# Score products of two attention maps as two half-height matmuls, in a one-core encoder layer

## The chip, the cores and the metric

The kernel runs on one NeuronCore of a Trainium2 chip; the other cores are idle. A core has TensorE (PE, matrix products; its weight loads are shown as PEld), VectorE (DVE), ScalarE (ACT), GpSimd (POOL) and SyncE (SP, which here only issues transfers). They run side by side, each through its own list of instructions in a fixed order, and wait for one another by semaphores. Matmul results land in PSUM, eight banks of 512 float32 columns for each of 128 partitions; everything else lies in SBUF, also with 128 partitions. The metric is the device time of one execution in microseconds (us), the median of several runs.

## The reference, cut to what matters

The program is one encoder layer on 1024 tokens of 1024 channels, in float32. A normalised input is projected to pooling channels and to queries, keys and values of 8 heads; a pooling branch and an attention branch are gated and merged, projected out and added; an MLP of width 4096 follows. The change lies in the attention branch, where each head has two softmax maps with their own 64-wide queries and keys and a common 128-wide value:

```python
qn = head_rmsnorm(q, g_q) * (HEAD_DIM ** -0.5)       # [.., 8 heads, 2 maps, 64]
kn = head_rmsnorm(k, g_k)
s = einsum('bqhid,bkhid->bihqk', qblk, kn)            # i: the map
s = where(allowed, s - slopes * dist, neg)            # block-causal, ALiBi
p = softmax(s, axis=-1)
a = p[:, 0] - lam * p[:, 1]
o = einsum('bhqk,bkhe->bqhe', a, vf)
```

## The kernel before, in words

**Digits.** Matrix products are made from fp32r operands, a rounded form of float32. To keep float32 accuracy, each operand is split into a high digit (a rounded copy, ScalarE) and a low digit (the rest, a VectorE or GpSimd subtraction). `mm3` (lines 114 to 119) adds up three products: high by high, high by low, low by high.

**Scores.** Map m of a head has 64 channels, and TensorE contracts over 128 rows, so a score product uses the rows twice. `stage_qkT` (444 to 466) transposes queries and keys of one tile of 128 tokens and puts digits on top of each other. For map 0, rows 0 to 63 are its own half and 64 to 127 the other; for map 1 it is the reverse. K holds the key's high digit on the own half (line 459) and its low digit on the other (460). Q holds two variants: variant 0 has the query's high digit on the own half (461) and its low digit on the other (462); variant 1 has the low digit on the own half (463) and the high digit on the other (464). One pass with variant 0 gives high by high plus low by low; a second with variant 1, into the same PSUM bank, gives low by high plus high by low.

`stage_scores` (468 to 517) goes over query tile t of head h. It has (t+1) x 128 keys, in chunks of up to 512, so one chunk for t below 4 and two above. For each map and each chunk it takes a PSUM bank `sc` (pool `ps_s`, two banks), runs the two passes (490 and 491), and evicts with one VectorE operation (493) which adds the distance penalty and keeps the running minimum. When all chunks of a map are there, ScalarE takes the exponential of the whole row (501). There are 8 heads, 8 tiles, 96 chunks, 192 score banks and 384 score matmuls. A chunk of 128 keys is streamed twice over, so the widths are 512, 384 and 256.

**Order.** The attention stage is a software pipeline. `ORDER` (48, 49) gives each stage an offset in steps; the loop at 636 to 655 takes one piece of each stage generator in turn and then runs them out. The pieces are QKV projection (A, `z`), normalisation (B), transposes (C, `tk`), scores (D, `sc`), transposes of the attention matrix (E, `ta`), the product with values (F, `po`), the small sums of squares (H) and a per-head norm (R, `trr`). The `yield` statements inside `stage_scores` set where its pieces end. Projections for gates (`g`) and pooling (`u`), written after the loop, serve as filler. The framework's scheduler then fixes each engine's list from these priorities and its own estimate of time; it may put other matmuls between two that stand next to each other in the source.

**What else uses part of the array.** Two kinds of matmul in this kernel have a weight of fewer than 128 rows or columns: the transposes of the small parameters at line 375 (`cols_ps`, 32 rows, once) and of the norm factors at line 602 (`trr`, 8 columns, once a head).

Of the kernel before, what the change touches and what calls it, by code (L numbers as in the profile page):

```python
# [11 lines left out]
AF = mybir.ActivationFunctionType  # L12
ALU = mybir.AluOpType
# [4 lines left out]
P = 128  # L18
# [5 lines left out]
HD = 64  # L24
# [4 lines left out]
BIG = 3.0e38  # L29
# [26 lines left out]
def encoder_kernel(  # L56
# [21 lines left out]
    nc = tc.nc  # L78
    x, out = x[0], out[0]
# [17 lines left out]
    def htile(shape, dt, name, th):  # L97
        return hpools[th].tile(shape, dt, tag="H", name=name)

    def ut(shape, dt, name):  # L100
        return up.tile(shape, dt, tag="U", name=name)
# [4 lines left out]
    def f(ap):  # L106
        return ap.bitcast(F32)
# [172 lines left out]
    with ExitStack() as ph:  # L280
# [83 lines left out]
        dist = sp.tile([P, S], F32, name="dist")  # L364
# [79 lines left out]
        def stage_qkT(h, t):  # L444

            th, c0 = t // 4, (t % 4) * P
            K, qn = KV[h][0][th], st[h, t]["qn"]
            tr = ps_t.tile([P, 512], F32, tag="tr", name=f"tk{h}_{t}")
            for i in range(2):
                nc.tensor.transpose(  # L450
                    tr[:, i * P : (i + 1) * P], qn[:, 2 * i : 2 * i + 2, :].rearrange("p a b -> p (a b)"), identf
                )
            Q = sp.tile([P, 2, 2, P], F32R, tag="Q", name=f"Q{h}_{t}", bufs=N_Q)
            halves = (slice(0, HD), slice(HD, P))
            for m in range(2):
                own, other = halves[m], halves[1 - m]
                q, k = tr[own, 0:P], tr[own, P : 2 * P]
                k_hi, q_hi = K[own, m, c0 : c0 + P], Q[own, m, 0, :]
                nc.scalar.copy(k_hi, k)
                nc.vector.tensor_tensor(K[other, m, c0 : c0 + P], k, f(k_hi), op=ALU.subtract)  # L460
                nc.scalar.copy(q_hi, q)  # L461
                nc.vector.tensor_tensor(Q[other, m, 0, :], q, f(q_hi), op=ALU.subtract)
                nc.vector.tensor_tensor(Q[own, m, 1, :], q, f(q_hi), op=ALU.subtract)  # L463
                nc.scalar.copy(Q[other, m, 1, :], q)  # L464
            st[h, t]["Q"] = Q
            yield

        def stage_scores(h, t):

            K, Q = KV[h][0], st[h, t]["Q"]  # L470
            n = (t + 1) * P
            if t < 4:
                sb = ut([P, 2, 512], F32, f"s{h}_{t}")
                s = [sb[:, 0, :], sb[:, 1, :]]
            else:
                s = [ut([P, S], F32, f"s{h}_{t}_{i}") for i in range(2)]
            nm = sp.tile([P, 2, 2], F32, tag="nm", name=f"nm{h}_{t}", bufs=3)
            Z = Zs[h]
            o0 = S - P - P * t
            for i in range(2):  # L480
                last = None
                for c in range(0, n, 512):
                    w = min(512, n - c)
                    sc = ps_s.tile([P, 512], F32, tag="sc", name=f"sc{h}_{t}_{i}_{c}")
                    rhs = K[c // 512][:, i, 0:w]
                    dst = sc[:, 0:w]
                    if w == P:
                        rhs = rhs.unsqueeze(1).broadcast_to([P, 2, P])
                        dst = sc[:, 0 : 2 * P].rearrange("p (a b) -> p a b", a=2)
                    nc.tensor.matmul(dst, Q[:, i, 0, :], rhs, start=True, stop=False)  # L490
                    nc.tensor.matmul(dst, Q[:, i, 1, :], rhs, start=False, stop=True)  # L491
                    acc = nm[:, i, c // 512 : c // 512 + 1]
                    nc.vector.tensor_tensor_reduce(  # L493
                        out=s[i][:, c : c + w], in0=sc[:, 0:w], in1=dist[:, o0 + c : o0 + c + w],
                        scale=2.0 ** -(h + 1), scalar=BIG if last is None else last,
                        op0=ALU.add, op1=ALU.min, accum_out=acc,
                    )
                    last = acc
                    if c + 512 < n:
                        yield  # L500
                nc.scalar.activation(  # L501
                    s[i][:, 0:n], s[i][:, 0:n], AF.Exp, bias=last, scale=-1.0, accum_out=Z[:, i, t : t + 1]
                )
                if i == 0:
                    yield

            cf = sp.tile([P, 1], F32, tag="cf", name=f"cf{h}_{t}", bufs=3)
            nc.vector.reciprocal(cf, Z[:, 1, t : t + 1])
            nc.vector.scalar_tensor_tensor(cf, cf, Z[:, 0, t : t + 1], nlam, op0=ALU.mult, op1=ALU.mult)
            nc.vector.scalar_tensor_tensor(  # L510
                s[0][:, 0:n], s[1][:, 0:n], cf, s[0][:, 0:n], op0=ALU.mult, op1=ALU.add
            )
            if (h, t) == (H - 1, NT - 1):

                nc.vector.tensor_scalar(zero, Z[:, 1, t : t + 1], 0.0, None, op0=ALU.mult)
            st[h, t]["a"] = s[0]
            yield
# [93 lines left out]
        def stage(w, g):  # L611
            h, t = divmod(g, NT)
            if w == "A":
                if t == 0:
                    head_start(h)
                yield from stage_qkv(h, t)
            elif w == "B":
                yield from stage_prep(h, t)
            elif w == "C":
                yield from stage_qkT(h, t)  # L620
            elif w == "D":
                yield from stage_scores(h, t)
            elif w == "E":
                yield from stage_aT(h, t)
            elif w == "F" and t % 2:
                yield from stage_pv(h, t // 2)
            elif w == "H" and t % 2:
                yield from stage_ssq(h, t // 2)
            elif w == "R" and t == NT - 1:
                yield from stage_norm(h)  # L630
            elif w == "W" and t == 0 and h:
                for kp in range(NK // 2):
                    load_w(h, kp)
                    split_w(h, kp, nc.gpsimd)

        for g in range(-2, N + 8):
# [11 lines left out]
            for tok in ORDER:  # L648
                if tok not in gens:
                    i = g - tok[1]  # L650
# [145 lines left out]
    for d in range(NK):  # L796
# [3 lines left out]
        for th in range(2):  # L800
# [5 lines left out]
            t = htile([P, 2, 512], F32R, f"mT{d}_{th}", th)  # L806
# [446 lines left out]
```

## Time and profile before

| | |
|---|---|
| median of 3 runs | 1582.8 us (1582.48 to 1592.09) |
| the profiled execution | 1589.36 us, its span 1587.6 us |
| granted TensorE clock | 0.992 of full speed |
| TensorE busy | 1551.9 us (98%) |
| VectorE busy | 1008.6 us (64%) |
| ScalarE busy | 812.1 us (51%) |
| GpSimd busy | 347.8 us (22%) |
| first score pass, line 490 | 192 matmuls |
| deleted VectorE line 462 | 128 operations, 37.0 us busy |

All rows but the first two come from one profiled execution. A span reaches from the first instruction to the last; the execution's own time is a little longer. A row of the order of time gives start, duration, engine, line, operation, output and inputs, then rows and columns of the weight (128*128), then the output's shape. Matmuls overlap on TensorE: the next starts before the one ahead has ended, so the time that a matmul takes from the engine is the distance from its start to the next one's, and the sum of durations is more than the time. A weight load (PEld) usually starts together with the matmul ahead of the one that it belongs to. Helper lines stand for many callers: L111 and L112 are the two halves of a split, L117 to L119 the three products of `mm3`; the tile names tell which.

### The profile page before, as it was taken

How to read it: one execution, taken by the hardware profiler on the slowest of the kernel's cores; microseconds unless marked ns; L12 is line 12 of the kernel's file. 1: busy time of each engine (PE TensorE's matmuls, PEld its weight loads, DVE VectorE, ACT ScalarE, POOL GpSimd, SP SyncE). 2: the span in 40 equal slices, each digit the busy share in tenths (PEclk: the TensorE clock that was granted, in tenths of full speed). 3: DMA queues.
4: the chain of work that ended last, by engine and by line, in shares of the span. 5: the costliest groups of instructions: out<-in, count | busy, mean ns of one | idle time of the engine just before them, and what ended most of it. 6: DMA issues, size and time to landing. Idle time of an engine off the chain costs nothing.

```text
span 1587.6 us, 21976 instructions
## 1 busy us (share of the span) xinstructions
PE 1551.9 (98%) x7649; PEld 1328.8 (84%) x7649; DVE 1008.6 (64%) x2265; ACT 812.1 (51%) x1776; POOL 347.8 (22%) x447
## 2 busy tenths in 40 slices
PE   7999999999999999998999998999999899999999
PEld 6998999999999989887888886888888678888887
DVE  6777777777878787645221468666666568545662
ACT  6656565655665565545332456555556533333331
POOL 5424242425343433212743100000000000000000
PEclk9999999999999999999999998999999999999999
DMA  7111111111111121258527334444434699536751
GB/s 224 51 53 54 54 54 56 43 54 57 53 58 52 57 74 57 81 177 273 153 83 216 138 124 128 163 149 153 157 121 152 234 353 354 166 119 225 218 174 39
DMA packets 166393, 206.41 MB, mean 130 GB/s; under 512 B 10037, under 2 KB 102922, under 8 KB 166282
## 3 DMA queue, kind: packets, MB, share of 16 engines
q1 hardware_dynamic: 148874, 177.71, 34.6%
q10 hardware_dynamic: 17408, 27.30, 4.6%
q8 instruction: 60, 0.98, 0.3%
q14 instruction: 51, 0.42, 0.1%
HBM read 150.42 MB, written 54.56 MB: 129 GB/s over the span
## 4 chain that ended last, share of the span: by engine, by line
PE 88%; DVE 4%; DMA 4%; ACT 1%; issue 1%; POOL 1%; SPq 1%; ACTq 0%; DVEq 0%; POOLq 0%
PE z L117 5%; PE z L119 5%; PE z L118 5%; PE Da L117 4%; PE Da L118 4%; PE Da L119 4%; PE g L118 3%; PE g L117 3%; PE g L119 3%; PE Db L118 3%; PE Db L119 3%; PE Db L117 3%; PE X L117 3%; PE X L118 3%; PE X L119 3%; PE sc L490 2%
## 5 line engine op out<-in xcount | busy, mean ns | idle before, releaser
L119 PE MATMUL z<-wqkv,hT 128*128 128x384 f32 x512 | 174.3, 341 | 0.7 <-DVE hT L112 0.7
L117 PE MATMUL z<-wqkv,hT 128*128 128x384 f32 x512 | 174.7, 341 | 0.4 <-DVE qn L432 0.3
L118 PE MATMUL z<-wqkv,hT 128*128 128x384 f32 x512 | 173.6, 339 | 0.0
L501 ACT ACTIVATE s<-s,nm 128x256 f32<-128x256 f32 (+7 forms) x128 | 99.6, 778 | 48.8 <-DVE nm L493 43.4
L240 POOL TENSOR_TENSOR ms<-ms,mhalf 128x4 f32<-128x4 f32 x64 | 67.6, 1056 | 157.6 <-DVE ms L239 138.5
L119 PE MATMUL g<-hT,fwgate 128*128 128x512 f32 x256 | 101.0, 394 | 0.0
L118 PE MATMUL g<-hT,fwgate 128*128 128x512 f32 x256 | 101.0, 394 | 0.0
L117 PE MATMUL g<-hT,fwgate 128*128 128x512 f32 x256 | 100.9, 395 | 0.0
L117 PEld LDWEIGHTS z<-wqkv,hT 128*128 128x128 f32 x512 | 96.8, 189 | 4.2 <-DVE qn L432 1.3
L119 PEld LDWEIGHTS z<-wqkv,hT 128*128 128x128 f32 x512 | 96.6, 189 | 3.4 <-DVE hT L112 1.5
L118 PEld LDWEIGHTS z<-wqkv,hT 128*128 128x128 f32 x512 | 96.8, 189 | 2.9
L493 DVE CUSTOM_DVE_ANT_0 s<-sc,dist 128x512 f32<-128x512 f32 (+3 forms) x128 | 74.7, 586 | 22.1 <-PE sc L491 20.7
L112 POOL TENSOR_TENSOR wqkv<-rqkv,wqkv 128x384 fp32r<-128x384 f32 x60 | 63.2, 1071 | 20.2 <-ACT wqkv L111 19.2
L490 PE MATMUL sc<-K,Q 128*128 128x512 f32 (+2 forms) x192 | 67.2, 355 | 0.1
L491 PE MATMUL sc<-K,Q 128*128 128x512 f32 (+2 forms) x192 | 66.6, 354 | 0.0
L112 DVE TENSOR_TENSOR AS<-s,AS 128x512 fp32r<-128x512 f32 x64 | 43.7, 689 | 31.4 <-ACT AS L111 31.4
L464 ACT CAST Q<-tk 64x128 fp32r<-64x128 f32 x128 | 33.2, 259 | 58.7 <-DVE Q L463 56.8
L438 POOL TENSOR_TENSOR qn<-qn,ggh 128x128 f32<-128x128 f32 x64 | 32.4, 506 | 137.6 <-DVE qn L432 119.4
L461 ACT CAST Q<-tk 64x128 fp32r<-64x128 f32 x128 | 33.0, 258 | 50.7 <-DVE K L460 49.2
L112 POOL TENSOR_TENSOR fwgate<-frgate,fwgate 128x512 fp32r<-128x512 f32 x32 | 45.3, 1418 | 53.0 <-ACT fwgate L111 52.9
L1009 ACT ACTIVATE u<-u 128x512 f32<-128x512 f32 x64 | 40.5, 632 | 31.4 <-DVE u L823 30.3
L119 PEld LDWEIGHTS g<-hT,fwgate 128*128 128x128 f32 x256 | 48.1, 188 | 8.6
(428 smaller groups left out, 4662.8 us busy)
## 6 DMA issues: line engine op xcount, KB each, us to landing
wd<-in_w_down_dram SPq DMA_DIRECT2D x56, 512.0 KB, 5.3
wu<-in_w_up_dram SPq DMA_DIRECT2D x32, 512.0 KB, 4.4
udS<-us SPq DMA_DIRECT2D x64, 256.0 KB, 2.1
ur<-udS SPq DMA_DIRECT2D x32, 512.0 KB, 3.4
rqkv<-in_w_in_dram SPq DMA_DIRECT2D x64, 192.0 KB, 3.0
ud<-u ACTq DMA_DIRECT2D x48, 256.0 KB, 2.0
ur<-ud SPq DMA_DIRECT2D x24, 512.0 KB, 8.3
frgate<-in_w_gate_dram SPq DMA_DIRECT2D x32, 256.0 KB, 2.8
```

Of the source, the lines that this page charges most:

```text
L112: (lo_eng or nc.vector).tensor_tensor(lo, src, f(hi), op=ALU.subtract)
L117: nc.tensor.matmul(ps, lhs_hi, rhs_hi, start=first, stop=False, **kw)
L118: nc.tensor.matmul(ps, lhs_hi, rhs_lo, start=False, stop=False, **kw)
L119: nc.tensor.matmul(ps, lhs_lo, rhs_hi, start=False, stop=last, **kw)
L240: nc.gpsimd.tensor_tensor(dst, dst, mhalf[:, :n], op=ALU.pow)
L461: nc.scalar.copy(q_hi, q)
L464: nc.scalar.copy(Q[other, m, 1, :], q)
L490: nc.tensor.matmul(dst, Q[:, i, 0, :], rhs, start=True, stop=False)
L491: nc.tensor.matmul(dst, Q[:, i, 1, :], rhs, start=False, stop=True)
L493: nc.vector.tensor_tensor_reduce(out=s[i][:, c : c + w], in0=sc[:, 0:w], in1=dist[:, o0 + c : o0 + c + w], scale=2.0 ** -(h + 1), scalar=B ...
L501: nc.scalar.activation(s[i][:, 0:n], s[i][:, 0:n], AF.Exp, bias=last, scale=-1.0, accum_out=Z[:, i, t : t + 1])
L1009: nc.scalar.activation(r, r, AF.Relu)
```

## The change

`stage_qkT` no longer writes the query's low digit on the other half of variant 0, so that half of the tile stays unused. `stage_scores` turns its loops inside out: for each chunk it takes both maps' PSUM banks, issues the high-by-high products of both maps as matmuls over 64 rows each (map 0 on rows 0 to 63, map 1 on rows 64 to 127), then both maps' full-height second passes, then both evictions. The product of the two low digits is no longer computed. The pieces of the generator change too: a piece now holds both maps of a chunk, and there is a `yield` after every chunk, the last included.

```diff
@@ stage_qkT
                 nc.scalar.copy(q_hi, q)
-                nc.vector.tensor_tensor(Q[other, m, 0, :], q, f(q_hi), op=ALU.subtract)
                 nc.vector.tensor_tensor(Q[own, m, 1, :], q, f(q_hi), op=ALU.subtract)
@@ stage_scores
-            for i in range(2):
-                last = None
-                for c in range(0, n, 512):
-                    w = min(512, n - c)
+            last = [None, None]
+            for c in range(0, n, 512):
+                w = min(512, n - c)
+                scs, rhs, dst = [], [], []
+                for i in range(2):
                     sc = ps_s.tile([P, 512], F32, tag="sc", name=f"sc{h}_{t}_{i}_{c}")
...
-                    nc.tensor.matmul(dst, Q[:, i, 0, :], rhs, start=True, stop=False)
-                    nc.tensor.matmul(dst, Q[:, i, 1, :], rhs, start=False, stop=True)
+                for i, own in enumerate((slice(0, HD), slice(HD, P))):
+                    nc.tensor.matmul(dst[i], Q[own, i, 0, :], rhs[i][own], start=True, stop=False)
+                for i in range(2):
+                    nc.tensor.matmul(dst[i], Q[:, i, 1, :], rhs[i], start=False, stop=True)
+                for i in range(2):
                     acc = nm[:, i, c // 512 : c // 512 + 1]
                     nc.vector.tensor_tensor_reduce(
...
-                    last = acc
-                    if c + 512 < n:
-                        yield
+                    last[i] = acc
+                yield
+            for i in range(2):
                 nc.scalar.activation(
-                    s[i][:, 0:n], s[i][:, 0:n], AF.Exp, bias=last, scale=-1.0, accum_out=Z[:, i, t : t + 1]
+                    s[i][:, 0:n], s[i][:, 0:n], AF.Exp, bias=last[i], scale=-1.0, accum_out=Z[:, i, t : t + 1]
                 )
```

In the changed file the half-height matmuls are line 494, the full-height ones 496, the evictions 499.

More of the change, by code (lines that the diff above doesn't have):

```diff
@@ L479, in stage_scores @@
             o0 = S - P - P * t
-            for i in range(2):
-                last = None
-                for c in range(0, n, 512):
-                    w = min(512, n - c)
+            last = [None, None]
[3 more added lines that the diff above has]
+                for i in range(2):
                     sc = ps_s.tile([P, 512], F32, tag="sc", name=f"sc{h}_{t}_{i}_{c}")
-                    rhs = K[c // 512][:, i, 0:w]
-                    dst = sc[:, 0:w]
+                    r, d = K[c // 512][:, i, 0:w], sc[:, 0:w]
@@ L487, in stage_scores @@
                     if w == P:
[L488 to L491, printed above, removed]
+                        r = r.unsqueeze(1).broadcast_to([P, 2, P])
+                        d = sc[:, 0 : 2 * P].rearrange("p (a b) -> p a b", a=2)
@@ L492, in stage_scores @@
+                    scs.append(sc)
+                    rhs.append(r)
+                    dst.append(d)
+                for i, own in enumerate((slice(0, HD), slice(HD, P))):
[3 more added lines that the diff above has]
+                for i in range(2):
                     acc = nm[:, i, c // 512 : c // 512 + 1]
@@ L493, in stage_scores @@
                     nc.vector.tensor_tensor_reduce(
-                        out=s[i][:, c : c + w], in0=sc[:, 0:w], in1=dist[:, o0 + c : o0 + c + w],
-                        scale=2.0 ** -(h + 1), scalar=BIG if last is None else last,
+                        out=s[i][:, c : c + w], in0=scs[i][:, 0:w], in1=dist[:, o0 + c : o0 + c + w],
+                        scale=2.0 ** -(h + 1), scalar=BIG if last[i] is None else last[i],
                         op0=ALU.add, op1=ALU.min, accum_out=acc,
                     )
-                    last = acc
```

## The prediction

> **What bounds the kernel now.** I read the page's summary and chain first, then a table of busy time by stretch over the attention stage, then the list of TensorE's own waits there, and last the order of time around single instructions.
>
> ```profile
> span 1587.6 us, 21976 instructions
> PE 1551.9 (98%) x7649; PEld 1328.8 (84%) x7649; DVE 1008.6 (64%) x2265; ACT 812.1 (51%) x1776; POOL 347.8 (22%) x447
> ...
> PE 88%; DVE 4%; DMA 4%; ACT 1%; issue 1%; POOL 1%; SPq 1%; ACTq 0%; DVEq 0%; POOLq 0%
> ```
>
> TensorE is busy 98% of the span and holds 88% of the chain that ended last. That is an average over stages, and the change touches one stage only, that of the score matmuls (first row below: count, shortest, median and longest in ns, first and last start in us). The row after it is the sum of seven stretches, 40 to 670 us; then come the only waits of TensorE of which the trace knows between 45 and 670 us (columns: total us, times, longest).
>
> ```profile
> L490 PE MATMUL sc<-K,Q x192: 276/389/501, 49.1 to 668.7; 128*128 128x512 f32 x96, 128*128 128x256 f32 x64, 128*128 128x384 f32 x32
> ```
>
> ```profile
> sum 630.00, PE 627.77 PEld 576.05 DVE 478.37 ACT 379.61 POOL 235.12; mean PE 89.68 PEld 82.29 DVE 68.34 ACT 54.23 POOL 33.59
> ```
>
> ```profile
> PE ta L546 <- DVE AT_0l L112: 0.9, 1, 0.9
> PE ta L546 <- DVE AT_4l L112: 0.6, 1, 0.6
> PE z L117 <- DVE qn L432: 0.3, 1, 0.3
> ```
>
> Of 630 us, TensorE is without work for 2.2 us, and its waits for others are 1.8 us. VectorE is busy 478 of the 630. So in this stage a microsecond more or less on TensorE is a microsecond of the end, and work taken from VectorE or ScalarE can give back no more than about 2 us.
>
> A busy row is not the price of a matmul, since one overlaps the next; the price is the distance from start to start. The page's order of time shows it (start, duration, line):
>
> ```profile
> 409.83 0.40 PE L118 MATMUL u<-hT,fwpool 128*128 128x512 f32 x1
> 410.06 0.28 PE L490 MATMUL sc<-K,Q 128*128 128x256 f32 x1
> 410.18 0.28 PE L491 MATMUL sc<-K,Q 128*128 128x256 f32 x1
> 410.30 0.40 PE L119 MATMUL u<-hT,fwpool 128*128 128x512 f32 x1
> 410.54 0.39 PE L117 MATMUL u<-hT,fwpool 128*128 128x512 f32 x1
> ```
>
> ```profile
> 402.19 0.33 PE L117 MATMUL z<-wqkv,hT 128*128 128x384 f32 x1
> 402.37 0.33 PE L118 MATMUL z<-wqkv,hT 128*128 128x384 f32 x1
> ```
>
> A 512-column matmul takes 0.23 us of TensorE, a 384-column one 0.18, a 256-column one 0.12.
>
> **The change, part by part.**
>
> *The first passes.* Groups of the first score pass by shape, and below them the VectorE operation that the change deletes:
>
> ```profile
> L490 PE MATMUL sc<-K,Q 128*128 128x512 f32 x96 | 38.9, 405 | 0.1
> L490 PE MATMUL sc<-K,Q 128*128 128x256 f32 x64 | 18.3, 285 | 0.0
> L490 PE MATMUL sc<-K,Q 128*128 128x384 f32 x32 | 10.9, 342 | 0.0
> ...
> L462 DVE TENSOR_TENSOR Q<-tk,Q 64x128 fp32r<-64x128 f32 x128 | 37.0, 289 | 20.2 <-ACT Q L461 17.1
> ```
>
> These 192 cost 96 x 0.23 + 32 x 0.18 + 64 x 0.12 = 35.5 us. Afterwards there are still 192, of the same widths, on half of the rows. A half-height matmul streams as many columns, so by itself it saves nothing; only two of them side by side save one, at most 17.7 us in all.
>
> Whether they stand side by side is decided by the scheduler, not by the source line. In the built program of the changed kernel TensorE's list reads, at a typical place (L494 is the half-height pass, L496 the full-height one; names are tile, map, chunk):
>
> ```
> L494 sc_5_0_0  128x512      map 0, half height
> L496 sc_5_0_0  128x512      map 0, full height
> L118, L119, L117, L118 z    128x384
> L494 sc_5_1_0  128x512      map 1, half height
> L496 sc_5_1_0  128x512
> ```
>
> I went through the whole list: in none of the 96 pairs is map 0's half-height matmul followed at once by map 1's of the same chunk. Three times map 1's stands next to map 0's of the following chunk (widths 256, 384 and 256 at the narrower one); that can save 0.12 + 0.18 + 0.12 = 0.4 us. The other 186 stand alone between full-height matmuls. So there are 189 excursions from the full array into the 64-row form and back; in the kernel before there is one such excursion by rows (32 rows, L375) and eight by columns (8 of 128, L602).
>
> *What an excursion costs.* The trace has one by rows. hps are transposes, cols_ps is the 32-row one, g the next full-height matmul; PEld rows are weight loads.
>
> ```profile
> 39.77 0.60 PE L266 MATMUL hps<-identf,hn 128*128 128x128 f32 x4
> ```
>
> ```profile
> 40.09 0.27 PE L266 MATMUL hps<-identf,hn 128*128 128x128 f32 x1
> ...
> 40.29 0.13 PEld L375 LDWEIGHTS cols_ps<-identf,rows 32*128 32x128 f32 x1 [0.17 <-issue]
> 40.30 0.24 PE L375 MATMUL cols_ps<-identf,rows 32*128 32x32 f32 x1
> ...
> 40.47 0.19 PEld L118 LDWEIGHTS g<-hT,fwgate 128*128 128x128 f32 x1
> 40.47 0.50 PE L118 MATMUL g<-hT,fwgate 128*128 128x512 f32 x1
> 40.57 0.19 PEld L119 LDWEIGHTS g<-hT,fwgate 128*128 128x128 f32 x1
> 40.80 0.39 PE L119 MATMUL g<-hT,fwgate 128*128 128x512 f32 x1
> ```
>
> Transposes follow each other at (0.60 - 0.27)/3 = 0.11 us. Elsewhere a weight load starts with the matmul ahead of it; here L375's starts 0.20 us after the last hps, 0.17 of it idle with nothing waited for, and L118's load starts 0.17 after L375's matmul, although both streams had work. L118's matmul truly begins at about 40.57, where the load behind it starts, 0.10 after its own load. From the last hps to L119 are 0.71 us; at the usual distances (0.11 + 0.11 + 0.23) they would be 0.45. **This excursion cost 0.26 us.**
>
> Among transposes the weight load is already in the open, half of each 0.11. Among wide matmuls it is hidden, and an excursion uncovers it twice. By steps: a transpose streams 128 columns in about 0.06 (a quarter of 0.23), so the load came 0.14 after the stream's end; then the matmul 0.01 (as recorded for L375) to 0.10 (as for L118) after its load. That makes 0.15 to 0.24 on the way in and 0.24 on the way out, 0.39 to 0.48; measured from the usual slot in place of the stream's end (0.09 late) it is 0.10 to 0.19 and 0.19, 0.29 to 0.38. The ends are 0.26 and 0.48; I take **0.36**, the middle, since three kinds of neighbour are mixed: 149 excursions follow ordinary wide matmuls, 35 transposes or the small sums, 5 a second score pass.
>
> The other bound is the column form, with eight cases and no loss at all (the first of them in PE rows, the count of all, then its PEld rows):
>
> ```profile
> 156.45 0.34 PE L118 MATMUL z<-wqkv,hT 128*128 128x384 f32 x1
> 156.63 0.27 PE L602 MATMUL trr<-identf,r 128*8 128x128 f32 x1
> 156.74 0.49 PE L546 MATMUL ta<-identf,s 128*128 128x128 f32 x3
> ```
>
> ```profile
> L602 PE MATMUL trr<-identf,r x8: 270/271/273, 156.6 to 702.6; 128*8 128x128 f32 x8
> ```
>
> ```profile
> 156.46 0.09 PEld L602 LDWEIGHTS trr<-identf,r 128*8 128x8 f32 x1
> 156.63 0.36 PEld L546 LDWEIGHTS ta<-identf,s 128*128 128x128 f32 x3
> ```
>
> The small load starts 0.01 after the matmul ahead of it, the next one with trr itself, and the distances are the usual 0.18 and 0.11; the other seven go the same way. So the floor is nothing, the ceiling 0.48. The half-height matmul is cut by rows like L375, so I go by that row. The Trainium skill's page "TensorEngine Tiling (Array Packing)", section Key Properties, says that a change of tiling mode, not only of tile, drains TensorE. This case's trace agrees for the 32-row form (0.17 us idle) and not for the 8-column one (0.01 us); by that sentence read for all forms the sum would stay as it is.
>
> *Sum.* 189 x 0.36 = 68.0 us more, less 0.4 for the three neighbours: **+67.6 us**. The profiled execution was 1589.4 us (span 1587.6 and 1.8 around it), which would become 1657; on the median of 1582.8, which the verdict uses, 1650.
>
> *VectorE's deleted operation.* 128 x 0.289 = 37 us leave an engine with 152 us free in this stage. TensorE has no wait that names Q, so I count nothing, at most 2 us. In a stage 68 us longer VectorE has more room still, so nothing there covers less than before.
>
> *Both maps' score banks at once.* There are two sc banks. In the source the four matmuls of a chunk now precede both evictions, so the next chunk's map 0 waits for an eviction:
>
> ```profile
> L493 DVE CUSTOM_DVE_ANT_0 s<-sc,dist 128x512 f32<-128x512 f32 x80 | 54.8, 686 | 8.0 <-PE sc L491 6.9
> ```
>
> The 32 tiles of more than 512 keys have a second chunk. As the list is built, z, g or po matmuls stand between the halves and cover an eviction of 0.69 us; uncovered it would be 32 x 0.69 = 22 us, with g, z and po queued behind it on TensorE. I take nothing. DMA queues are as before: the change issues no transfer and moves none past another.
>
> **The rivals.**
>
> *Free switch (not slower).* A 64-row weight load is pulled ahead as trr's was, and the 64-row matmul fits between its neighbours. Then TensorE does the same 0.23, 0.18 and 0.12 slots as before: 1582.8 - 0.4 and up to 2 for VectorE, 1580 to 1583. For it speak the eight trr rows; against it the one row case, which is the nearer shape. It decides from the switch: below 16/189 = 0.08 us an excursion, the change is inside 1%.
>
> *Side by side (faster).* If halves ran together and switches were free, 17.7 us would go: 1565. The Trainium skill's "TensorE: Matmul & The Clock Gate", section "Measured speedup vs the span model", gives for tiles in different row groups one matmul's time plus about 4 ns each; no run here shows that yet. In this kernel it needs neighbours, and the list has three.
>
> *Small switch.* 64 rows drain less than 32 rows did, 0.08 to 0.24 us: 1598 to 1628.
>
> *Larger switch or bank waits.* Drain of 0.36 and the 22 us of evictions, or a drain of over 0.48 because the full load time (0.19 in the rows) stands in the open: 1672 to 1690.
>
> **How the numbers follow.** Drain by rows, 0.26 to 0.48 an excursion (1632 to 1673): 0.66. Small switch (1598 to 1628): 0.12. Free switch: 0.11. Larger: 0.08. Side by side: 0.03. A range of 1605 to 1680 holds the first, most of the small switch and part of the larger one, some 0.8. This kernel's measurement tells about 1% (16 us) from no change. Faster by over 1%: side by side, 0.03. Within: the free switch, 0.11. Slower: the rest, 0.86.
>
> **What would show it.** Right: L494's weight load starts 0.3 to 0.4 us after the matmul ahead of it, not with it; the load after L494 likewise; the start-to-start distance around an L494 of 512 columns is 0.5 to 0.7 us for the two steps where it was 0.46; the stage's stretch to the last score is some 68 us longer and the rest as long as before; VectorE's busy time is 37 us less. Wrong: loads of L494 that start with the matmul ahead; a stage of the same length; TensorE waits on L499's evictions (VectorE s) of more than a few us.

## The result, and the profile after

The changed kernel takes 1661.8 us (1661.3 to 1662.0) where the kernel before takes 1582.7 us: a ratio of 1.0485, 95% interval 1.0456 to 1.0513. It is 79 us slower. The profiled executions, 1661.34 and 1589.36 us, differ by 72 us, because that of before lies 7 us above its own median.

The summary of the changed kernel's page:

```profile
span 1659.6 us, 21851 instructions
PE 1619.9 (98%) x7649; PEld 1326.5 (80%) x7649; DVE 962.2 (58%) x2137; ACT 815.9 (49%) x1776; POOL 343.0 (21%) x447
```

TensorE has as many matmuls as before and is again "98% busy", 68 us more of it. That row can't tell work from a switch: a matmul that lasts longer counts as busy (a first pass of 512 columns 0.49 us in the rows below, 0.40 in the mean of before). The row of the weight loads (PEld) can: its busy time stayed (1328.8 us before, 1326.5 now) while the span grew, so its share fell from 84% to 80%. VectorE lost 128 instructions and 46 us, 37 of them those of line 462.

Next, one stretch of each kernel, from 40 us to the first matmul of the next stage (`bp`, which starts at 701.5 us before and at 777.1 us after); first the kernel before, then the changed one. The columns are the stretch, its length, and busy time with the number of instructions for each engine.

```profile
40.00:701.50 661.50, 659.27 (x3773) 602.66 (x3772) 493.65 (x1564) 397.00 (x1137) 240.28 (x328) 1.00 0.19 60
```

```profile
40.00:777.00 737.00, 734.27 (x3768) 602.59 (x3768) 444.39 (x1430) 399.96 (x1133) 236.28 (x327) 1.00 0.17 54
```

The same matmuls (both pages count 7649; the few that differ here fell over the edge of the stretch), with the same weight-load time to 0.1 us, at the same clock, take 75.5 us longer. The rest of the program, from the first `bp` to the end, went from 886.1 to 882.5 us. So the loss lies in the attention stage alone.

Inside the stage it shows up in the weight loads' idle time. From the list of waits of the changed kernel (total us, times, longest):

```profile
PEld sc L494 <- issue: 22.3, 90, 0.4
PEld sc L496 <- issue: 14.9, 65, 0.4
```

"Issue" means that the trace knows of nothing that was waited for. The two rows hold 155 of these gaps; the others stand in small rows under the names of other engines, so the price is read from single places. One place, in order of time, TensorE first and its weight loads second:

```profile
258.08 0.34 PE L117 MATMUL z<-wqkv,hT 128*128 128x384 f32 x1
258.25 0.34 PE L118 MATMUL z<-wqkv,hT 128*128 128x384 f32 x1
258.52 0.49 PE L494 MATMUL sc<-K,Q 64*128 64x512 f32 x1
258.94 0.50 PE L496 MATMUL sc<-K,Q 128*128 128x512 f32 x1
259.28 0.28 PE L117 MATMUL po<-AT_0h,V 128*128 128x256 f32 x1
```

```profile
258.08 0.19 PEld L118 LDWEIGHTS z<-wqkv,hT 128*128 128x128 f32 x1
258.52 0.18 PEld L494 LDWEIGHTS sc<-K,Q 64*128 64x128 f32 x1 [0.25 <-issue]
258.94 0.19 PEld L496 LDWEIGHTS sc<-K,Q 128*128 128x128 f32 x1 [0.24 <-issue]
259.05 0.19 PEld L117 LDWEIGHTS po<-AT_0h,V 128*128 128x128 f32 x1
```

L118's load starts with L117's matmul, as everywhere. L494's does not start with L118's matmul at 258.25 but at 258.52, and L496's not with L494's but 0.42 later. L496's matmul begins in truth at 259.05, where the load behind it starts. From 258.25 to 259.05 are 0.80 us; a 384-column and a 512-column matmul take 0.17 + 0.23 = 0.40. The excursion cost 0.40 us.

Nearly all of the 186 single excursions look like this: 163 cost 0.38 to 0.42 us, and 17 cost more than 0.45. Sorted by the width of the matmul ahead (128, 256, 384, 512) and of the half-height one (256, 384, 512), the medians of the twelve kinds lie between 0.39 and 0.40 us, worked out from the starts in the trace as above. The load into the 64-row form comes 0.09 us after its usual slot, the load back 0.19 us after its own, and the matmul 0.11 us after that load. In that measure 189 excursions are 74 to 76 us, where the stage grew by 75.5.

### The profile page after: what moved, and what is told of

Same layout as the page of the kernel before. It is cut to its first block, busy times and chain, and to the rows that moved or that the text cites. A ratio compares the mean times of both kernels' runs of the same rounds, so it can differ in the third digit from the quotient of the medians.

```text
span 1659.6 us, 21851 instructions
## 1 busy us (share of the span) xinstructions
PE 1619.9 (98%) x7649; PEld 1326.5 (80%) x7649; DVE 962.2 (58%) x2137; ACT 815.9 (49%) x1776; POOL 343.0 (21%) x447
## 4 chain that ended last, share of the span: by engine, by line
PE 50%; DMA 3%; DVE 2%; ACT 1%; issue 1%; POOL 0%; ACTq 0%; DVEq 0%; POOLq 0%
PE Da L117 4%; PE Da L119 4%; PE Da L118 3%; PE X L117 3%; PE Db L117 3%; PE Db L119 3%; PE X L118 3%; PE X L119 3%; PE Db L118 3%; PE ba L119 2%; PE ba L117 2%; PE ba L118 2%; PE op L117 2%; PE op L118 2%; PE op L119 2%; PE Z L118 2%
## 5 line engine op out<-in xcount | busy, mean ns | idle before, releaser
L117 PE MATMUL z<-wqkv,hT 128*128 128x384 f32 x512 | 176.7, 345 | 0.1
L118 PE MATMUL z<-wqkv,hT 128*128 128x384 f32 x512 | 175.6, 343 | 0.0
L499 DVE CUSTOM_DVE_ANT_0 s<-sc,dist 128x512 f32<-128x512 f32 (+3 forms) x128 | 74.7, 587 | 57.0 <-PE sc L496 55.3
L117 PE MATMUL g<-hT,fwgate 128*128 128x512 f32 x256 | 101.2, 396 | 1.2 <-ACT u L707 0.7
L118 PEld LDWEIGHTS z<-wqkv,hT 128*128 128x128 f32 x512 | 96.9, 189 | 5.8 <-issue 2.4
L117 PEld LDWEIGHTS z<-wqkv,hT 128*128 128x128 f32 x512 | 96.9, 189 | 5.5 <-issue 2.5
L118 PE MATMUL g<-hT,fwgate 128*128 128x512 f32 x256 | 101.1, 395 | 0.0
L494 PE MATMUL sc<-K,Q 64*128 64x512 f32 (+2 forms) x192 | 85.0, 450 | 0.0
L496 PE MATMUL sc<-K,Q 128*128 128x512 f32 (+2 forms) x192 | 80.9, 421 | 0.0
L494 PEld LDWEIGHTS sc<-K,Q 64*128 64x128 f32 x192 | 34.6, 184 | 45.2 <-issue 22.3
L117 PEld LDWEIGHTS g<-hT,fwgate 128*128 128x128 f32 x256 | 48.1, 188 | 10.5 <-ACT u L707 1.0
L499 DVE CUSTOM_DVE_ANT_0 s<-sc,dist,nm 128x128 f32<-128x128 f32 (+3 forms) x64 | 35.1, 549 | 36.3 <-PE sc L496 35.9
```

Source lines behind the costliest of these rows:

```text
L117: nc.tensor.matmul(ps, lhs_hi, rhs_hi, start=first, stop=False, **kw)
L118: nc.tensor.matmul(ps, lhs_hi, rhs_lo, start=False, stop=False, **kw)
L494: nc.tensor.matmul(dst[i], Q[own, i, 0, :], rhs[i][own], start=True, stop=False)
L496: nc.tensor.matmul(dst[i], Q[:, i, 1, :], rhs[i], start=False, stop=True)
L499: nc.vector.tensor_tensor_reduce(out=s[i][:, c : c + w], in0=scs[i][:, 0:w], in1=dist[:, o0 + c : o0 + c + w], scale=2.0 ** -(h + 1), scal ...
```

## The experiments

**The height alone.** Before's loops and order stay, only the first pass is cut.

```diff
-                nc.vector.tensor_tensor(Q[other, m, 0, :], q, f(q_hi), op=ALU.subtract)
...
-                    nc.tensor.matmul(dst, Q[:, i, 0, :], rhs, start=True, stop=False)
+                    own = (slice(0, HD), slice(HD, P))[i]
+                    nc.tensor.matmul(dst, Q[own, i, 0, :], rhs[own], start=True, stop=False)
```

> Before's loops and order kept; only the first pass is cut to 64 rows and VectorE's line 462 is deleted, so the low-by-low product is not computed. The built list has 186 excursions into the 64-row form (180 single matmuls, 6 times two neighbours). Theory (each excursion costs about 0.40 us of TensorE, as between 258.25 and 259.05 us of the changed kernel's trace): 186 x 0.40 = 74 us, less about 1 for the neighbours, so about 1656 us (1648 to 1662). Rival (the new loop order, two banks taken at once and other ends of the generator's pieces, is what costs): 1580 to 1590 us.

Measured: 1655.7 us, 1.0467 of before (1.045 to 1.0485), +72 us, as the theory has it. The single excursions of its trace have a median of 0.39 us. The six neighbours saved nothing, though 1 us had been expected: both matmuls are of map 0, on the same 64 rows, and one follows the other.

**The order alone.** The changed kernel's loops with full-height first passes.

```diff
+                nc.vector.tensor_tensor(Q[other, m, 0, :], q, f(q_hi), op=ALU.subtract)
...
-                for i, own in enumerate((slice(0, HD), slice(HD, P))):
-                    nc.tensor.matmul(dst[i], Q[own, i, 0, :], rhs[i][own], start=True, stop=False)
+                for i in range(2):
+                    nc.tensor.matmul(dst[i], Q[:, i, 0, :], rhs[i], start=True, stop=False)
```

> The changed kernel's loops and order, but every first pass at full height and line 462 back. No 64-row matmul is left. Theory: within 5 us of 1582.7, since the order is only moved and VectorE's 37 us are covered. Rival (the order costs): 1640 us and more, with TensorE waits on the score evictions.

Measured: 1588.7 us, 1.0036 (1.001 to 1.0061), +5 us with an interval of 2 to 10, at the edge of what was expected. The waits of the rival are not there: up to 700 us the score matmuls wait 0.3 us for an eviction. The order is not free, but it is a small part. Where its 5 us lie is not shown, since the profiled executions of the two kernels (1587.87 and 1589.36 us) don't differ that way. Together the two edits would give 72 + 5 = 77 us; both at once gave 79.

**Fewer rows without the other form.** Map 0's first pass contracts over 96 of 128 rows.

```diff
-                    nc.tensor.matmul(dst, Q[:, i, 0, :], rhs, start=True, stop=False)
+                    own = (slice(0, 96), slice(0, P))[i]
+                    nc.tensor.matmul(dst, Q[own, i, 0, :], rhs[own], start=True, stop=False)
```

> Before's order; map 0's first pass over rows 0 to 95 in place of 0 to 127 (half of its low-by-low product is left out), which the built program still issues in the full 128 x 128 form. Theory (the change of form costs, not the smaller height): 1583 us, within 3. Rival (fewer rows are slower by themselves): a share of the 79 us for 96 of 192 matmuls, about 1600 to 1622 us.

Measured: 1582.9 us, ratio 1.000 (0.9985 to 1.0016). One such matmul and the loads around it:

```profile
382.90 0.34 PE L119 MATMUL z<-wqkv,hT 128*128 128x384 f32 x1
383.07 0.40 PE L491 MATMUL sc<-K,Q 96*128 96x512 f32 x1
383.31 0.34 PE L117 MATMUL z<-wqkv,hT 128*128 128x384 f32 x1
```

```profile
382.90 0.19 PEld L491 LDWEIGHTS sc<-K,Q 96*128 96x128 f32 x1
383.08 0.19 PEld L117 LDWEIGHTS z<-wqkv,hT 128*128 128x128 f32 x1
```

Both loads start with the matmul ahead, and the 512 columns take 0.24 us from start to start, as at 128 rows (0.23 to 0.24). A matmul over 96 rows, in the full form, is neither faster nor slower; it is not the smaller height as such that costs.

**Half the dose.** Only map 0 is cut to 64 rows.

```diff
-                nc.vector.tensor_tensor(Q[other, m, 0, :], q, f(q_hi), op=ALU.subtract)
+                if m == 1:
+                    nc.vector.tensor_tensor(Q[other, m, 0, :], q, f(q_hi), op=ALU.subtract)
...
-                    nc.tensor.matmul(dst, Q[:, i, 0, :], rhs, start=True, stop=False)
+                    own = (slice(0, HD), slice(0, P))[i]
+                    nc.tensor.matmul(dst, Q[own, i, 0, :], rhs[own], start=True, stop=False)
```

> Before's order; only map 0's first pass is cut to 64 rows, map 1's keeps 128 and its line 462 (map 0's low-by-low product is left out). The built list has 84 excursions (72 single matmuls, 12 times two of map 0 in a row, which use the same rows and can't stand side by side). Theory (0.40 us an excursion, as measured around 180 of the height_only run and 186 of the changed kernel): 84 x 0.40 = 34 us, about 1617 us (1612 to 1622). Rival (a cost for each half-height matmul, not for each excursion): 96 x 0.40 = 38 us, 1621 us. Rival (a threshold, all or nothing): 1583 or 1656.

Measured: 1620.9 us, 1.0239 (1.0209 to 1.0268): +38 us, interval 33 to 42, about half of height_only's 72. A threshold is out. Between 84 excursions (34 us) and 96 matmuls (38 us) the time doesn't decide; the trace does. In the twelve doubles both matmuls use the same 64 rows and follow one another; here is one of them, TensorE and then its loads:

```profile
167.27 0.34 PE L119 MATMUL z<-wqkv,hT 128*128 128x384 f32 x1
167.53 0.61 PE L492 MATMUL sc<-K,Q 64*128 64x512 f32 x2
168.08 0.39 PE L117 MATMUL po<-AT_0h,V 128*128 128x256 f32 x1
```

```profile
167.53 0.29 PEld L492 LDWEIGHTS sc<-K,Q 64*128 64x128 f32 x2 [0.25 <-issue]
168.08 0.19 PEld L117 LDWEIGHTS po<-AT_0h,V 128*128 128x128 f32 x1 [0.25 <-issue]
168.19 0.19 PEld L117 LDWEIGHTS z<-wqkv,hT 128*128 128x128 f32 x1
```

There is one gap into the form and one out of it. From 167.27 to 168.19 are 0.92 us; the three matmuls (384, 512 and 256 columns) take 0.17 + 0.23 + 0.12 = 0.52 by their usual slots, and 0.40 is left, as for a single one. The price is one of the excursion, not of the half-height matmul.

**Pairs held together by a critical section.** The two half-height matmuls were put into a block which the scheduler keeps whole.

```diff
+                with tc.tile_critical():
+                    for i, own in enumerate((slice(0, HD), slice(HD, P))):
+                        nc.tensor.matmul(dst[i], Q[own, i, 0, :], rhs[i][own], start=True, stop=False)
```

> The changed kernel with both maps' half-height matmuls held together, so that the scheduler puts nothing between them: 96 excursions, each with two matmuls side by side. Theory: 96 x 0.40 = 38 us for the excursions, less 17.7 us for the first passes that run beside another: +21, about 1603 us (1596 to 1612); more if both banks must be free at once and TensorE waits for evictions, up to 22 us more. Rival (what costs is the height or the order, not the number of excursions): about 1660 us as the changed kernel. Rival (two row halves do not run side by side): 1621 us.

Measured: 1702.5 us, 1.0755 (1.0731 to 1.0778). None of the theories said this. The waits of the weight loads, and one pair:

```profile
PEld sc L495 <- issue: 83.0, 96, 3.6
PEld ta L553 <- issue: 17.9, 29, 5.4
```

```profile
291.63 0.39 PE L118 MATMUL u<-hT,fwpool 128*128 128x512 f32 x1
292.45 0.50 PE L495 MATMUL sc<-K,Q 64*128 64x512 f32 x2 [0.44 <-ACT Q L461]
293.19 0.41 PE L553 MATMUL ta<-identf,s 128*128 128x128 f32 x2 [0.23 <-ACT Q L463]
```

The pair does run side by side (two in 0.50 us), but 0.82 us pass ahead of it and 0.74 to the next matmul. The trace has a branch of TensorE's sequencer ahead of the block and an instruction called DRAIN behind it, 96 times each. So the time of this run measures the block and not the pairs; of its rivals it answers one, for the two row halves do run side by side.

**Pairs made ready together, and their control.** Both maps' banks are one tile of two banks, so that they come free together, and an order without a wait keeps both half-height matmuls behind the last step of Q. (The start of the kernel, which borrows the same banks, uses the first half of such a tile.)

```diff
-        ps_s = ph.enter_context(tc.tile_pool(name="ps_s", bufs=N_S, space=PSUM))
+        ps_s = ph.enter_context(tc.tile_pool(name="ps_s", bufs=1, space=PSUM))
...
+                both = ps_s.tile([P, 2, 512], F32, tag="sc", name=f"sc{h}_{t}_{c}")
                 for i in range(2):
-                    sc = ps_s.tile([P, 512], F32, tag="sc", name=f"sc{h}_{t}_{i}_{c}")
+                    sc = both[:, i, :]
...
+                    tc.add_manual_dep(
+                        half.ins, made[h, t].ins.name,
+                        mybir.DependencyInfo(mybir.DependencyClass.NoSync, mybir.DependencyReason.DATA),
+                        reason="pair",
+                    )
```

> The changed kernel with both maps' score banks taken as one tile of two banks, so that both half-height matmuls become ready together, and with map 0's held back to the end of the preparation of Q by an order without a wait. No branch and no added wait on TensorE. The built list has 94 of 96 pairs next to each other, 98 excursions in all. Theory: 98 x 0.40 = 39 us, less 94/96 x 17.7 = 17.3 us: +22, about 1605 us (1598 to 1612), plus what the two banks cost by themselves (see twobank_full). Rival (a pair costs 0.8 us and more, as in pairs_kept): 1660 to 1700 us. Rival (the pair pays for itself, as the source intends): 1575 to 1583 us.

The control has the same edit, with first passes over all 128 rows and line 462 back:

> The control of pairs_by_bank: the same two-bank tile and the same order, with first passes at full height and line 462 back, so no excursion at all. Theory: 1583 to 1592 us; what it is above 1583 is the price of taking both banks at once, and pairs_by_bank is 22 us (17 to 27) above this run. Rival (two banks at once make TensorE wait for evictions): 1600 us and more.

Measured: pairs_by_bank 1619.0 us, 1.0213 (1.017 to 1.0256); twobank_full 1608.4 us, 1.0159 (1.0131 to 1.0186). Two banks at once cost 26 us by themselves, more than I had expected; the time is that of the rival, 1600 us and more, but not for its reason. Up to 700 us the score matmuls wait 1.3 us for evictions. The loss shows behind that, in this row of twobank_full:

```profile
700.00:790.00 90.00, 75.38 (x333) 61.97 (x333) 41.91 (x78) 42.60 (x75) 27.34 (x23) 0.89 0.59 194
```

In the kernel before, TensorE is busy 85.94 us of the same 90, at a granted clock of 0.96 in place of 0.89. With two banks at once the last score starts at 709 us (669 before), and no gate matmul is left behind it (122 before), so nothing fills the waits for the last heads' attention. Over the whole span TensorE is without work for 53 us (36 before); these 17 us are most of the 22 by which the two profiled spans differ.

The pairs add 10.5 us to that, less than the expected 17 to 27. The two intervals (7 and 4 us either way) allow some 2 to 19, so at best the lower end of it. One pair of pairs_by_bank, TensorE and then its loads:

```profile
285.28 0.34 PE L118 MATMUL z<-wqkv,hT 128*128 128x384 f32 x1
285.54 0.51 PE L497 MATMUL sc<-K,Q 64*128 64x512 f32 x2
285.98 0.74 PE L504 MATMUL sc<-K,Q 128*128 128x512 f32 x2
```

```profile
285.54 0.19 PEld L497 LDWEIGHTS sc<-K,Q 64*128 64x128 f32 x2 [0.25 <-DVE AT L112]
285.98 0.30 PEld L504 LDWEIGHTS sc<-K,Q 128*128 128x128 f32 x2 [0.25 <-issue]
```

Both half-height loads fit into 0.19 us and the load of L504 comes 0.44 after them, where behind a single one it came 0.42 after. The pair costs one matmul and one excursion: 0.23 + 0.40 = 0.63 us. Two full-height passes cost 0.46. With 384 columns it is 0.58 against 0.35, with 256 it is 0.52 against 0.24. So **even a perfect pair loses**, 0.17 to 0.28 us each; over the 94 pairs of this trace that is 20 us of TensorE. The end shows only half of it, since the control loses time that the pairs' run doesn't: away from the excursions, between 40 and 800 us, the distances from start to start exceed the usual slots by some 34 us in all in twobank_full and by some 22 in pairs_by_bank. With two banks at once this stage is no longer bound by TensorE everywhere. Why pairs_by_bank waits less is not shown; besides the pairs it differs from its control by line 462, 45 us less work for VectorE.

No version beat the kernel before. By these prices an excursion would have to save more than 0.40 us to gain, that is hold two pairs of 512 columns, which needs four score banks, two more than there are. That is an estimate; it was not tried.

## Why the prediction was right

The forecast was 1650 us, in a range of 1605 to 1680; measured were 1661.8, +79 us in place of +68.

**The bound.** It was read right: TensorE was full in this stage, and the stage became longer by what TensorE lost. VectorE's 46 us less brought nothing that shows.

**The list decides, not the source.** Right. In none of the 96 pairs do the halves stand together; the order of the source was no promise. The three neighbours did run side by side:

```profile
502.18 0.34 PE L117 MATMUL z<-wqkv,hT 128*128 128x384 f32 x1
502.45 0.50 PE L494 MATMUL sc<-K,Q 64*128 64x512 f32 x2
502.88 0.39 PE L496 MATMUL sc<-K,Q 128*128 128x256 f32 x1
```

The page "TensorE: Matmul & The Clock Gate" of the Trainium skill, section "Measured speedup vs the span model", has tiles in different row groups run at once, some 4 ns apart; these rows and those of pairs_by_bank agree (the two starts are 4 ns apart here, 3 ns in the median of the 94 pairs). The rival "side by side" failed on the two conditions that it named, neighbours and a free switch.

**The price of an excursion.** The mechanism was right, the size a little low: 0.36 forecast, 0.40 measured, and 189 x 0.04 = 7.6 us is the larger part of the difference between +68 and +79. The prediction had two readings of the one 32-row case, 0.29 to 0.38 from the usual slot and 0.39 to 0.48 from the stream's end, and took the middle. The first reading was the right one, at its upper end: the load into the form is 0.09 us late (0.09 there), the load out of it late by as much again, and each time another 0.10 to 0.11 us pass from the load to its matmul. For the half-height load I had let that be as short as 0.01; in the doubles of map0_half the second load starts 0.11 us after the first, and that is where the first matmul truly begins. The bound from the column form was no bound for rows. That one case of 32 rows would give the price of 64 was a guess; nothing in the trace of before could show it, and it held.

**The signs.** The load of L494 comes 0.27 us after the matmul ahead of it in the place shown, and 0.33 in the median behind 512 columns; 0.3 to 0.4 had been named. The load after it comes 0.42 us later at 512 columns. Both are late, as forecast, and the sizes are a little off.

**The order.** Counted at nothing, 5 us measured (2 to 10). It may be the other part of the difference, but the interval of the result itself is 72 to 81 us, and the traces don't show it.

**Free switch, small switch.** Both are refuted by the 0.39 to 0.40 us of all twelve kinds.

**Bank waits.** Right at nothing. TensorE's waits in the changed kernel between 45 and 745 us:

```profile
PE g L117 <- ACT u L707: 0.7, 1, 0.7
PE yp L117 <- ACT go L742: 0.7, 2, 0.5
PE tk L450 <- DVE AT_0l L112: 0.4, 1, 0.4
PE g L117 <- ACT yps L734: 0.4, 1, 0.4
```

They are 2.2 us, and none is on a score's eviction (L499). In twobank_full, where both banks are taken and freed as one, there was a price of 26 us, but little of it as waits on evictions.

**Where it was wrong: the place.** The prediction said that the stretch to the last score would grow by some 68 us. The last score starts at 708.8 us, 40 us later than before. The rest lies behind it, in gate matmuls (`g`), first before, then after:

```profile
669.00:702.00 33.00, 29.00 (x122) 22.41 (x122) 3.78 (x6) 1.00 0.52 159
```

```profile
709.00:778.00 69.00, 62.04 (x264) 48.84 (x264) 6.76 (x10) 1.00 0.34 115
```

142 gate matmuls more stand behind the last score, at 0.23 us 33 us. They are filler, and the scheduler put fewer of them between the scores. The stage as a whole grew by 75.6 us all the same, since on a full engine it does not matter where the filler stands.

## What to carry to other kernels

Before splitting a matmul by rows, look in a trace for the nearest case of such a matmul, and read when the weight loads around it start: a load that doesn't start with the matmul ahead is the price, here 0.40 us an excursion, whatever the widths (256 to 512 columns). A half-height matmul saves nothing alone, and a pair saves one matmul (0.23 us at 512 columns), so a pair between full-height matmuls loses; only a longer stay in the form could pay, which no run here tried. Where a scheduler makes the list, count neighbours in the built list, and count excursions, before counting savings.

## What the runs showed of the hardware

- The cost of going into the 64-row form and back is 0.39 to 0.40 us in the medians of twelve combinations of widths, so it is a fixed time and not a share of a matmul. Two matmuls in a row on the same 64 rows pay it once.
- A matmul over 96 rows costs nothing extra (1582.9 us with 96 of them), and the eight 8-column transposes in the trace of before cost nothing either, while 64 rows (0.40 us) and 32 rows (0.26 us, one case, among transposes) do. So not every small weight costs; of the cases seen, those with 64 or 32 rows do.
- Two row halves side by side, of 512 columns each, last as long as one (0.44 us from load to load against 0.42).
